# GpSimd makes the operands of the first merged projection alone: hi, lo and sums for 16 units beside attention heads 4 to 7

## The chip, the core and the metric

One core of one Trainium2 chip runs the whole program. The metric is device time in microseconds (us), the median of three runs; the profile is one more execution of the same program. The engines are TensorE (PE; its weight loads are PEld), VectorE (DVE), ScalarE (ACT), GpSimd (POOL) and the queue engine SyncE (SP). Each runs its own list of instructions strictly in order and waits for the others by semaphores.

## The reference

One encoder layer is applied to two groups of 512 tokens (g = 0, 1) with shared weights, model width 1024, all in float32. Cut to the part around the change:

```
h   = rmsnorm(x, g_mix);  u = h @ w_in          # columns feed both branches and the gates
hm  = mlstm(...)                                # 4 heads, both directions
y_m = (sigmoid(o) * rmsnorm(hm)) @ w_mo         # "first merged projection"
y_a = softmax_attention(q, k, v) @ w_ao         # 8 heads, 128 + 64 wide scores
x   = x + (sigmoid(g_m) * y_m + sigmoid(g_a) * y_a) @ w_out
x   = x + (silu(h2 @ w_gate) * (h2 @ w_up)) @ w_down ;  x = x + sigmoid(x @ w_ple_gate) * (p @ w_ple)
```

## The kernel before, in words

Every large product is made of float32 parts: an operand is split into a rounded part `hi` (a cast, on ScalarE) and the rest `lo` (operand minus hi, on VectorE, helper `lo_of`, L152), and three matmuls hi·hi, hi·lo, lo·hi are added up. A tile is 128 partitions by 512 columns.

The stages in order are: the first projection with the mLSTM heads, the attention (8 heads; each head is done for g = 0 and then g = 1, called half-heads here), then a chain of merged projections (w_mo, then w_ao), w_out, the gated network and the end. In the attention a half-head has, for four blocks of 128 queries, scores (`sc`, L742 to L746), a row maximum on VectorE (L748), an exponential on ScalarE (L751), a scaling of `p` (L754 on ScalarE, L756 on VectorE for one block in four), transposes (`pt`, L759), the split of the transposed block (`aph` on ScalarE, L761; `apl` on VectorE), and then the product with v (`av`, L766 to L768). Beside it stands the preparation of the same half-head of the next head: projections (`pj`), the rotary part on VectorE for every second head (`rope`, L691 to L698, then L723 and L724), the splits of q, k (`qnl`, `knl`) and of v, whose lo part (`vnl`) runs on GpSimd.

A merged projection multiplies a 2 by 2 block matrix of weights with a 2 by 2 block matrix of operands (`a`, `b` for one half of the channels in the two groups, `c`, `d` for the other half) in seven products instead of eight. The class `Ops` makes the operands of the products P1 (a), P2 (c), P7 (b - d), P6 (b - d - a), P5, Q4 and P3, for k = 0 to 3 in each. One (product, k) is called a unit. `Ops.need` makes a unit: `part` gives the source (a load of `hzd`, for P7 and P6 with a subtraction, L805 and L808), then hi, then lo (L827 to L830). For the first merged projection the 16 units of P1, P2, P7, P6 are made inside the attention: `HOPS` says how many after each half-head (3 after each of heads 4 and 5, 2 after each of head 6), and the loop at L968 draws them from the list `units`. Their raw tiles go through four buffers (two of `H`, tag rs, and two of `EV`, tag bk). The other twelve units (P5, Q4, P3) come when the chain starts; their raw tiles (again 16 loads of `hzd`) go to the pool `X2`, which opens in head 7. `Seven` makes the weights of the seven products: it loads two weight blocks from ScalarE's queue (`wst`), makes sums on GpSimd (L869 to L879) and splits them (`wp`, L843 and L152). The function `chain` asks for weights and operands a few products ahead.

The order on each engine isn't the order of the code: outside of pinned stretches a scheduler sets it when the program is built, from the dependences and its own estimates, and the pools decide which buffer a load has to wait for.

Of the kernel before, what the change touches and what calls it, by code (L numbers as in the profile page):

```python
# [62 lines left out]
def encoder_kernel(ctx: ExitStack, tc: tile.TileContext, a):  # L63
# [3 lines left out]
    class Engine:  # L67


        def __init__(self, e):  # L70
            self.e = e
# [13 lines left out]
    V, S, E, GP = (Engine(e) for e in (nc.vector, nc.scalar, nc.tensor, nc.gpsimd))  # L85
# [65 lines left out]
    def lo_of(out, src, hi, e=V):  # L151
        e.tensor_tensor(out=out, in0=src, in1=hi.bitcast(F32), op=ALU.subtract)  # L152
# [183 lines left out]
    for g in range(G):  # L336
# [3 lines left out]
        for d in range(2):  # L340
            for i in range(2):
                lo = 64 + 32 * i + 4 * d
# [74 lines left out]
    for i in range(NB):  # L417
        c = slice(i * P, (i + 1) * P)
        V.tensor_tensor_scan(
            out=M[:, c], data0=A[0][:, c], data1=A[0][:, c], initial=mprev[:, i : i + 1], op0=ALU.max, op1=ALU.max  # L420
# [4 lines left out]
    for d in range(1, NB):  # L425
        GP.tensor_copy(out=A[d][:, (NB - d) * P : T], in_=A[0][:, (NB - d) * P : T])
        for j in range(NB - d):
            e = (j + d) * P - 1
            V.tensor_scalar(
                out=A[d][:, j * P : (j + 1) * P],  # L430
# [13 lines left out]
    for d in range(NB + 1):  # L444
        src = A[d] if d < NB else em
# [196 lines left out]
    def merge_gate(name, dst, c):  # L642
        w = w8(f"{name}{c}")
        for g in range(G):
            t = hproj(w, g, EV("bk", "tg"))
            S.activation(out=t, in_=t, func=AF.Tanh, scale=0.5)
            nc.sync.dma_start(dst[g][c], t)
# [20 lines left out]
    for half in range(2):  # L668
        whi, wlo = weight(a["wv"][half])
        for g in range(G):  # L670
            for i in range(NB):
                bk = bank()
                for k in range(2):
                    n = slice(T * k, T * k + T)
                    hi, lo = (x[:, i * P : (i + 1) * P] for x in lat["ckv"][g][k])
# [40 lines left out]
    def attn_proj(hd, g, wa):  # L716
        if hd % 2 == 0:
            r = rope(proj1(wa, lat["cq"][g], 2, 0, "pj"), 4)
            st0 = Q("qst", "qs0", F32R)
            st1 = Q("qst", "qs1", F32R)  # L720
            S.copy(st0[0:64], r[0:64])
            S.copy(st1[64:128], r[64:128])
            V.tensor_tensor(out=st0[64:128], in0=r[0:64], in1=st0[0:64].bitcast(F32), op=ALU.subtract)  # L723
            V.tensor_tensor(out=st1[0:64], in0=r[64:128], in1=st1[64:128].bitcast(F32), op=ALU.subtract)  # L724
            qst[g] = [st0, st1]
        qn = split(proj1(wa, lat["cq"][g], 2, 256, "pj"), Q, "qkv", "qn")
        kn = split(proj1(wa, lat["ckv"][g], 2, 512, "pj"), Q, "qkv", "kn")
        vt = Q("tr", "avt")
        c = hd % 4 * P
        nc.sync.dma_start(vt.rearrange("p (a b) -> p a b", a=NB), vd[g][hd // 4].rearrange("a p c -> p a c")[:, :, c : c + P])  # L730
        vn = split(vt, Q, "qkv", "vn", GP)
        return qn, kn, vn, qst[g][hd % 2]
# [50 lines left out]
    def op(name, n, dt):  # L783
        return (H if name in ("P1", "P2", "P7", "P6") else late["OP"])("h", n, dt)

    class Ops:
# [1 line left out]


        def __init__(self, raw, tmp, sums):  # L790
            self.raw, self.tmp, self.sums = raw, tmp, sums
            self.r, self.t, self.x = {}, {}, {}

        def get(self, n, k):
# [26 lines left out]
        def need(self, name, ks=range(4)):  # L821
            x = self.x.setdefault(name, [])
            for k in ks:
                if len(x) == k:
                    src = self.part(name, k)
                    hi = op(name, "xh", F32R)
                    S.copy(hi, src)  # L827
                    lo = op(name, "xl", F32R)
                    lo_of(lo, src, hi)
                    x.append((hi, lo))  # L830

    wpn, wsn = [0], [0]
# [124 lines left out]
        raws[0] += 1  # L957
        return load(hzd[g][k], *stage[raws[0] % 4])

    hops = Ops(hraw, None, lambda n: V if n == "P7" else GP)  # L960
    hops.tmp = lambda: None
    units = [(n, [k]) for k in range(4) for n in ("P1", "P2", "P7", "P6")]

# [4 lines left out]
    for hd in range(AH):  # L968
# [7 lines left out]
        for g in range(G):  # L976
            attn(hd, g, ops[g])
            if hd < AH - 1:
                ops[g] = attn_proj(hd + 1, g, wa)
            for _ in range(HOPS.get((hd, g), 0)):  # L980
                hops.need(*units.pop(0))
        for _ in range(BULK[2 + hd]):
            merge_gate(*bulk.pop(0))
    assert not bulk
    Q.close()
    late["OP"] = Slots("OP", h=24, sg=4, ev=8)

# [34 lines left out]
    for g in range(G):  # L1022
        for k in (0, 4, 1, 5, 2, 6, 3, 7):
            t = yr[g][k]
            hi = H("h", "yh", F32R)
            S.activation(out=hi, in_=t, func=AF.Copy, scale=0.5)
            lo = H("h", "yl", F32R)
# [304 lines left out]


LEAD = 2
HOPS = {(4, 0): 3, (4, 1): 3, (5, 0): 3, (5, 1): 3, (6, 0): 2, (6, 1): 2}
LATN = (3, 0)
BULK = [10, 2, 1, 1, 1, 1, 0, 0, 0, 0]

# [92 lines left out]
```

## Time and profile before

| | us |
|---|---|
| median of 3 runs (lowest, highest) | 1901.08 (1899.88, 1902.36) |
| the profiled execution's own time | 1901.91 |
| its span, first to last instruction | 1900.0 |
| PE busy | 1843.9 (97% of the span) |
| DVE busy | 1235.4 (65%) |
| ACT busy | 879.3 (46%) |
| POOL busy | 466.8 (25%) |
| mean granted TensorE clock | 0.993 |

Busy is the time in which an engine had an instruction running. PE is close to full over the whole span, so time can only be lost or won where it stands idle or where its clock is lowered; idle time of the other engines costs nothing by itself. The sixteen units lie between about 740 and 790 us of the span, the attention ends and the merged chain begins at about 868 us.

### The profile page before, as it was taken

What the parts mean: (1) busy time and instruction counts of PE and PEld (TensorE: products, weight loads), DVE (VectorE), ACT (ScalarE), POOL (GpSimd) and SP (SyncE); (2) the same over time, 40 slices, a digit from 0 to 9 for tenths busy, and PEclk for the clock granted to TensorE, in tenths of its full rate; (3) what the DMA queues carried; (4) which work ended last, traced back from release to release, by engine and by line L of the source; (5) the groups of instructions that cost most, each with busy time, mean ns of one, the idle gap of its engine ahead of it and who ended that gap; (6) DMA issues with size and microseconds to landing.
All of it is one profiled execution on the core that took longest, in us unless ns stands there. A gap on an engine that the chain in (4) does not pass through costs nothing.

```text
span 1900.0 us, 24519 instructions
## 1 busy us (share of the span) xinstructions
PE 1843.9 (97%) x8840; PEld 1534.3 (81%) x8840; DVE 1235.4 (65%) x2153; ACT 879.3 (46%) x1711; POOL 466.8 (25%) x334
## 2 busy tenths in 40 slices
PE   7999999999999998999999998999999999999997
PEld 6888998988888877777877887888888887887886
DVE  7656575836556567976897586444444558878757
ACT  5255554644444565775534355333333344434442
POOL 3000000100000000233350035666465652322100
PEclk9999999999999999999999999999999999999998
DMA  4111111112253113345555241232223346534232
GB/s 164 51 45 34 57 34 56 34 67 73 78 177 133 57 64 117 102 142 201 162 193 183 89 167 60 90 123 99 97 98 102 120 142 228 162 127 136 89 126 89
DMA packets 98169, 207.59 MB, mean 109 GB/s; under 512 B 10688, under 2 KB 21312, under 8 KB 98048
## 3 DMA queue, kind: packets, MB, share of 16 engines
q1 hardware_dynamic: 85952, 163.03, 25.5%
q10 hardware_dynamic: 12096, 43.00, 7.0%
q8 instruction: 69, 1.13, 0.2%
q14 instruction: 52, 0.43, 0.1%
HBM read 151.89 MB, written 54.10 MB: 108 GB/s over the span
## 4 chain that ended last, share of the span: by engine, by line
PE 84%; DVE 10%; ACT 3%; DMA 2%; issue 2%; SPq 0%; DVEq 0%; ACTq 0%
PE b L894 12%; PE b L896 12%; PE b L895 12%; PE mm L183 8%; PE mm L181 8%; PE mm L182 8%; PE nm L580 3%; PE mm L79 2%; DVE xl L152 2%; PE mm L495 2%; PE mm L497 2%; PE mm L496 2%; DVE wp L152 1%; PE mm L1241 1%; PE mm L1243 1%
## 5 line engine op out<-in xcount | busy, mean ns | idle before, releaser
L894 PE MATMUL b<-xh,wp 128*128 128x512 f32 x1148 | 443.1, 394 | 9.9 <-ACT wp L843 4.4
L896 PE MATMUL b<-xh,wp 128*128 128x512 f32 x1148 | 445.0, 392 | 7.6 <-DVE wp L152 7.6
L895 PE MATMUL b<-xl,wp 128*128 128x512 f32 x1148 | 448.9, 392 | 0.0
L843 ACT CAST wp<-wst 128x512 fp32r<-128x512 f32 (+1 forms) x270 | 164.1, 612 | 307.5 <-PE b L896 251.4
L152 DVE TENSOR_TENSOR wp<-wst,wp 128x512 fp32r<-128x512 f32 (+1 forms) x270 | 239.4, 888 | 76.2 <-ACT wp L843 75.9
L894 PEld LDWEIGHTS b<-xh,wp 128*128 128x128 f32 x1148 | 216.5, 189 | 63.1 <-ACT wp L843 9.0
L896 PEld LDWEIGHTS b<-xh,wp 128*128 128x128 f32 x1148 | 216.6, 189 | 56.1 <-DVE wp L152 8.9
L895 PEld LDWEIGHTS b<-xl,wp 128*128 128x128 f32 x1148 | 216.5, 189 | 46.3
L181 PE MATMUL mm<-hh,whi 128*128 128x512 f32 x592 | 233.1, 394 | 7.3 <-ACT whi L166 7.0
L183 PE MATMUL mm<-hh,wlo 128*128 128x512 f32 x592 | 232.7, 395 | 2.3 <-DVE wlo L152 2.2
L182 PE MATMUL mm<-hl,whi 128*128 128x512 f32 x592 | 233.1, 394 | 0.3 <-DVE hl L277 0.3
L869 POOL TENSOR_TENSOR s<-wst,wst 128x512 f32<-128x512 f32 (+1 forms) x42 | 64.8, 1543 | 426.1 <-DMA wst<-w 171.6
L934 DVE TENSOR_TENSOR u<-b,u 128x512 f32<-128x512 f32 x90 | 61.5, 688 | 144.4 <-PE b L896 88.1
L181 PEld LDWEIGHTS mm<-hh,whi 128*128 128x128 f32 x592 | 112.4, 190 | 31.0 <-ACT whi L166 7.0
L183 PEld LDWEIGHTS mm<-hh,wlo 128*128 128x128 f32 x592 | 112.2, 190 | 26.4 <-DVE wlo L152 3.4
L182 PEld LDWEIGHTS mm<-hl,whi 128*128 128x128 f32 x592 | 112.2, 189 | 24.0 <-DVE hl L277 0.9
L166 ACT CAST whi<-wst 128x1024 fp32r<-128x1024 f32 (+1 forms) x71 | 73.0, 1029 | 104.3 <-PE mm L182 68.9
L152 DVE TENSOR_TENSOR xl<-ld,xh 128x512 fp32r<-128x512 f32 x121 | 94.9, 813 | 11.7 <-ACT xh L1176 6.8
L152 DVE TENSOR_TENSOR wlo<-wst,whi 128x1024 fp32r<-128x1024 f32 (+1 forms) x71 | 87.0, 1226 | 23.4 <-ACT whi L166 23.1
L929 ACT COPY u<-b 128x512 f32<-128x512 f32 x90 | 50.8, 588 | 107.6 <-PE b L896 80.2
L152 POOL TENSOR_TENSOR vnl<-avt,vnh 128x512 fp32r<-128x512 f32 x16 | 21.4, 1335 | 306.5 <-ACT vnh L156 283.8
L872 POOL TENSOR_TENSOR wst<-wst,wst 128x512 f32<-128x512 f32 (+1 forms) x42 | 78.6, 1873 | 39.2 <-DVE wp L152 29.9
(338 smaller groups left out, 3567.1 us busy)
## 6 DMA issues: line engine op xcount, KB each, us to landing
wst<-w SPq DMA_DIRECT2D x75, 512.0 KB
wst<-w ACTq DMA_DIRECT2D x60, 512.0 KB
ld<-actd SPq DMA_DIRECT2D x77, 256.0 KB
actd<-t SPq DMA_DIRECT2D x44, 256.0 KB
actd<-sg SPq DMA_DIRECT2D x33, 256.0 KB
x<-x SPq DMA_DIRECT2D x32, 256.0 KB
ld<-hzd SPq DMA_DIRECT2D x32, 256.0 KB
wst<-wd ACTq DMA_DIRECT2D x16, 512.0 KB
```

What stands on the lines that cost most here:

```text
L152: e.tensor_tensor(out=out, in0=src, in1=hi.bitcast(F32), op=ALU.subtract)
L166: S.copy(hi[:, :n], st[:, :n])
L181: E.matmul(bk, whi[:, c], hi, start=k == 0, stop=False)
L182: E.matmul(bk, whi[:, c], lo, start=False, stop=False)
L183: last_mm[0] = E.matmul(bk, wlo[:, c], hi, start=False, stop=k == nk - 1)
L843: S.copy(hi, src)
L869: GP.tensor_tensor(out=src, in0=a11, in1=a21, op=ALU.add)
L872: GP.tensor_tensor(out=a11, in0=a11, in1=a21, op=ALU.add)
L894: E.matmul(bk, whi[:, c], hi, start=bool(first) and k == 0, stop=False, **sk)
L895: E.matmul(bk, whi[:, c], lo, start=False, stop=False, **sk)
L896: E.matmul(bk, wlo[:, c], hi, start=False, stop=k == self.kh - 1, **sk)
L934: V.tensor_tensor(out=t, in0=b, in1=t, op=ALU.add if name == "P2" else ALU.subtract)
```

## The change

`Ops` gets a field `parts`. Where it names an engine, that engine makes both hi (as a copy with a cast) and lo; for the first merged projection it is GpSimd, which also takes the subtraction of P7 that VectorE had. The sixteen units are spread as two per half-head over heads 4 to 7, eight times two. Before the chain starts the field is taken back and the raw tiles are forgotten, so P5, Q4 and P3 use ScalarE and VectorE as before. Since the loop switches the loads to `X2` in head 7, the four units of k = 3 now read from `X2` too.

```
         def __init__(self, raw, tmp, sums):
-            self.raw, self.tmp, self.sums = raw, tmp, sums
+            self.raw, self.tmp, self.sums, self.parts = raw, tmp, sums, None
...
                     hi = op(name, "xh", F32R)
-                    S.copy(hi, src)
+                    if self.parts:
+                        self.parts.tensor_copy(out=hi, in_=src)
+                    else:
+                        S.copy(hi, src)
                     lo = op(name, "xl", F32R)
-                    lo_of(lo, src, hi)
+                    lo_of(lo, src, hi, self.parts or V)
...
-    hops = Ops(hraw, None, lambda n: V if n == "P7" else GP)
+    hops = Ops(hraw, None, lambda n: GP)
+    hops.parts = GP
...
     assert not bulk
+    hops.parts, hops.r, hops.t = None, {}, {}
...
-HOPS = {(4, 0): 3, (4, 1): 3, (5, 0): 3, (5, 1): 3, (6, 0): 2, (6, 1): 2}
+HOPS = {(hd, g): 2 for hd in range(4, 8) for g in range(2)}
```

VectorE before, at the start of the units (`xl` is the lo part of a unit, `ld` its raw tile, `apl` and `mx` belong to the attention, `rp` and `rs` to rope):

```order
L152 TENSOR_TENSOR xl_7482<-ld_7478,xh_7480 128x512
L749 TENSOR_SCALAR mx_7197<-mx_7197 128x1
L752 RECIPROCAL mx_7177<-mx_7177 128x1
L152 TENSOR_TENSOR knl_7121<-pj_7112,knh_7119 128x512
L805 TENSOR_TENSOR ld_7484<-ld_7484,ld_7486 128x512
L152 TENSOR_TENSOR xl_7491<-ld_7484,xh_7489 128x512
L152 TENSOR_TENSOR apl_7130<-pt_7144,aph_7129 128x4x128
L752 RECIPROCAL mx_7197<-mx_7197 128x1
L691 TENSOR_TENSOR rp_7234<-pj_7227,cos 128x512
L695 TENSOR_TENSOR rs_7236<-pj_7227,sin 32x512 x4
L152 TENSOR_TENSOR apl_7130<-pt_7164,aph_7129 128x4x128
```

VectorE now, at the same place:

```order
L752 RECIPROCAL mx_7177<-mx_7177 128x1
L749 TENSOR_SCALAR mx_7197<-mx_7197 128x1
L152 TENSOR_TENSOR knl_7121<-pj_7112,knh_7119 128x512
L152 TENSOR_TENSOR apl_7130<-pt_7144,aph_7129 128x4x128
L752 RECIPROCAL mx_7197<-mx_7197 128x1
L152 TENSOR_TENSOR apl_7130<-pt_7164,aph_7129 128x4x128
L691 TENSOR_TENSOR rp_7234<-pj_7227,cos 128x512
L695 TENSOR_TENSOR rs_7236<-pj_7227,sin 32x512 x4
```

The subtraction L805 and the lo parts that stood ahead of the attention's `apl` and of rope are gone from VectorE's list.

GpSimd before, at the end of the attention (`vnl` of the last half-head, then sums for P5, L811, and Q4, L817 and L818):

```order
L152 TENSOR_TENSOR vnl_8244<-avt_8240,vnh_8242 128x512
L811 TENSOR_TENSOR ld_8533<-ld_8533,ld_8535 128x512
L817 TENSOR_TENSOR ld_8582<-ld_8582,ld_8506 128x512
L817 TENSOR_TENSOR ld_8592<-ld_8592,ld_8515 128x512
L817 TENSOR_TENSOR ld_8602<-ld_8602,ld_8524 128x512
L818 TENSOR_TENSOR ld_8582<-ld_8582,ld_8585 128x512
L817 TENSOR_TENSOR ld_8612<-ld_8612,ld_8533 128x512
L818 TENSOR_TENSOR ld_8592<-ld_8592,ld_8595 128x512
L818 TENSOR_TENSOR ld_8602<-ld_8602,ld_8605 128x512
L818 TENSOR_TENSOR ld_8612<-ld_8612,ld_8615 128x512
L879 TENSOR_TENSOR wst_8622<-wst_8622 128x512
```

GpSimd now, the last part of the same stretch (`xl_8453` is P7 for k = 3, `ld_8446` its raw tile, `xh_8456` and `xl_8458` are P6 for k = 3):

```order
L152 TENSOR_TENSOR xl_8453<-ld_8446,xh_8451 128x512
L817 TENSOR_TENSOR ld_8612<-ld_8612,ld_8533 128x512
L818 TENSOR_TENSOR ld_8582<-ld_8582,ld_8585 128x512
L818 TENSOR_TENSOR ld_8592<-ld_8592,ld_8595 128x512
L818 TENSOR_TENSOR ld_8602<-ld_8602,ld_8605 128x512
L808 TENSOR_TENSOR ld_8446<-ld_8446,ld_8336 128x512
L818 TENSOR_TENSOR ld_8612<-ld_8612,ld_8615 128x512
L828 CAST xh_8456<-ld_8446 128x512
L882 TENSOR_TENSOR wst_8622<-wst_8622 128x512
L152 TENSOR_TENSOR xl_8458<-ld_8446,xh_8456 128x512
```

Between the `vnl` of the last half-head and the last Q4 sum (`ld_8612` by L818) there were 8 instructions; now there are 19, seven of them for the k = 3 units.

ScalarE before, in the first products of the chain (`u` copies a bank out; `wp` is the hi part of a weight, `wp_8802` that of P1 in the third pair of blocks; `wst_8780` its weight load):

```order
L827 CAST xh_8674<-ld_8615 128x512
L929 COPY u_8642<-b_1493_8491 128x512
L843 CAST wp_8744<-s_1556_8741 128x512
L855 DMA wst_8780<-w 128x1024
L929 COPY u_8660<-b_1538_8647 128x512
L843 CAST wp_8761<-wst_8484 128x512
L855 DMA wst_8782<-w 128x1024
L929 COPY u_8693<-b_1493_8491 128x512
L843 CAST wp_8785<-wst_8622 128x512
L843 CAST wp_8802<-wst_8780 128x512
```

ScalarE now, at the same place (`xh_8618` is the hi part of Q4 for k = 3, made from `ld_8612`):

```order
L830 CAST xh_8618<-ld_8612 128x512
L830 CAST xh_8662<-ld_8585 128x512
L858 DMA wst_8780<-w 128x1024
L830 CAST xh_8666<-ld_8595 128x512
L830 CAST xh_8670<-ld_8605 128x512
L830 CAST xh_8674<-ld_8615 128x512
L846 CAST wp_8761<-wst_8484 128x512
L858 DMA wst_8782<-w 128x1024
L846 CAST wp_8802<-wst_8780 128x512
L932 COPY u_8642<-b_1493_8491 128x512
```

The cast `wp_8802`, which needs the load `wst_8780`, now stands ahead of three `u` copies that it followed before; on PE its first matmul is the 73rd of the chain instead of the 133rd.

## Rows read from the trace of the kernel before

**Rows 1.** Windows: start:end, length, busy of each engine (instructions), granted clock, DMA share, GB/s.

```profile
743.00:867.00 124.00, 109.02 (x521) 85.23 (x520) 98.91 (x205) 90.55 (x187) 40.65 (x31) 0.99 0.37 120
743.00:760.00 17.00, 10.83 (x52) 8.03 (x51) 12.62 (x23) 9.89 (x21) 2.55 (x2) 1.00 0.50 151
760.00:769.00 9.00, 9.00 (x38) 7.30 (x37) 8.74 (x17) 6.65 (x15) 1.40 (x1) 0.81 0.59 177
761.00:762.00 1.00, 1.00 (x4) 0.81 (x3) 0.94 (x4) 0.93 (x2) 0.00 (x0) 0.50 0.50 104
769.00:777.00 8.00, 4.71 (x24) 3.36 (x23) 6.80 (x13) 6.38 (x14) 5.50 (x4) 1.00 0.35 110
800.00:850.00 50.00, 47.32 (x230) 37.35 (x229) 39.74 (x88) 37.88 (x79) 11.75 (x9) 1.00 0.28 97
867.00:900.00 33.00, 33.00 (x146) 27.19 (x145) 24.81 (x32) 15.78 (x29) 7.63 (x5) 1.00 0.69 248
```

**Rows 2.** Timeline, PE: start, length, instruction, [idle before it, and who released it].

```profile
750.07 0.50 PE L742 MATMUL sc<-knh,qnh 128*128 128x512 f32 x1 [1.69 <-ACT p L751]
...
759.24 0.50 PE L181 MATMUL pj<-ckvh,whi 128*128 128x512 f32 x1 [2.02 <-DVE mx L749]
...
775.54 0.66 PE L759 MATMUL pt<-ident,p 128*128 128x128 f32 x4 [1.94 <-ACT p L754]
...
815.83 0.50 PE L181 MATMUL pj<-cqh,whi 128*128 128x512 f32 x1 [1.08 <-DVE rs L695]
```

**Rows 3.** Timeline, DVE and ACT, units that wait for their load.

```profile
747.02 0.69 DVE L805 TENSOR_TENSOR ld<-ld,ld 128x512 f32<-128x512 f32 x1 [3.00 <-DMA ld<-hzd]
...
770.32 0.81 DVE L805 TENSOR_TENSOR ld<-ld,ld 128x512 f32<-128x512 f32 x1 [1.20 <-DMA ld<-hzd]
...
747.75 0.62 ACT L827 CAST xh<-ld 128x512 fp32r<-128x512 f32 x1 [3.32 <-DVE ld L805]
```

**Rows 4.** Groups by line and form, 690 to 860 us: busy, mean ns, idle before.

```profile
L152 DVE TENSOR_TENSOR xl<-ld,xh 128x512 fp32r<-128x512 f32 x16 | 10.7, 680 | 0.9 <-ACT xh L827 0.9
L805 DVE TENSOR_TENSOR ld<-ld,ld 128x512 f32<-128x512 f32 x4 | 2.9, 718 | 4.2 <-DMA ld<-hzd 4.2
L827 ACT CAST xh<-ld 128x512 fp32r<-128x512 f32 x16 | 9.6, 623 | 6.0 <-DVE ld L805 3.3 <-DVE wlo L152 2.2 <-DMA ld<-hzd 0.5
```

**Rows 5.** Timeline, POOL and DVE at the same time, and alone.

```profile
762.85 1.40 POOL L808 TENSOR_TENSOR ld<-ld,ld 128x512 f32<-128x512 f32 x1 [12.41 <-DVE xl L152]
...
763.03 2.03 DVE L152 TENSOR_TENSOR wlo<-wst,whi 128x768 fp32r<-128x768 f32 x1
...
789.80 0.96 DVE L152 TENSOR_TENSOR wlo<-wst,whi 128x768 fp32r<-128x768 f32 x1 [0.56 <-ACT whi L166]
...
749.17 1.28 POOL L808 TENSOR_TENSOR ld<-ld,ld 128x512 f32<-128x512 f32 x1 [3.39 <-DVE xl L152]
...
750.13 0.67 DVE L691 TENSOR_TENSOR rp<-pj,cos 128x512 f32<-128x512 f32 x1
```

**Rows 6.** Groups by line and form, POOL, whole span.

```profile
L808 POOL TENSOR_TENSOR ld<-ld,ld 128x512 f32<-128x512 f32 x4 | 5.2, 1310 | 19.3 <-DVE xl L152 15.8 <-DVE mx L749 1.9 <-issue 1.6
...
L426 POOL COPY A<-A 64x384 f32<-64x384 f32 x1 | 0.5, 498 | 0.0
```

**Rows 7.** Timeline of ACT, POOL, PE where the attention ends.

```profile
848.02 0.61 ACT L156 CAST vnh<-avt 128x512 fp32r<-128x512 f32 x1
...
852.53 3.78 POOL L817 TENSOR_TENSOR ld<-ld,ld 128x512 f32<-128x512 f32 x3
...
867.68 0.39 PE L894 MATMUL b<-xh,wp 128*128 128x512 f32 x1
...
879.93 0.34 ACTq L855 DMA_DIRECT2D wst<-w  x1
...
883.45 0.33 ACTq L855 DMA_DIRECT2D wst<-w  x1
...
888.62 1.44 POOL L869 TENSOR_TENSOR s<-wst,wst 128x512 f32<-128x512 f32 x1 [11.07 <-DMA wst<-w]
```

## The prediction

> **What bounds the kernel now.** I read the busy shares first: PE is busy 97% of the span, so the change can only act where PE is idle or slowed. I then cut the attention's second half into windows. From 743 to 867 us PE is busy 109.02 of 124.00, so 15.0 us are idle there, and in the chain behind it, 867 to 900, none of 33.00 [rows 1]. The idle time is not even. 743 to 760 loses 17.00 - 10.83 = 6.2 us and 769 to 777 loses 8.00 - 4.71 = 3.3 us: 9.5 us of the 15.0 lie in the 34 us where the units are made. 800 to 850 has the same attention work without units and loses 50.00 - 47.32 = 2.7 us [rows 1]. Between the two bad windows, 760 to 769, PE is never idle and yet does little: the granted clock is 0.81 on average and 0.50 at 761, the lower of its two levels (1.2 of 2.4 GHz), right after the idle spell [rows 1].
>
> The PE timeline then says who ended the waits: ScalarE's exponential (1.69 us at 750), VectorE's small steps (2.02 us at 759), ScalarE's scaling of p (1.94 us at 775) [rows 2]. Both engines had been held up by units. At 744 VectorE stood 3.00 us at the subtraction L805 because its load had not landed; ScalarE stood 3.32 us at the cast of the same unit, with the attention's next exponential behind it; at 769 the same happens for 1.20 us [rows 3]. What was queued behind then ran late, together with rope and further lo parts. So what bounds this stretch is VectorE and ScalarE working in order through instructions that are not urgent.
>
> **The change, part by part.** Taken off VectorE: 16 lo parts, 10.7 us, and 4 subtractions, 2.9 us, with 4.2 us of standing for loads. Taken off ScalarE: 16 casts, 9.6 us, with 6.0 us of standing [rows 4]. The number of `hzd` loads stays. For PE the gain is read from the two windows: 9.5 us idle, less what is idle without units. The hop-free rate is 2.7 us in 50, for 34 us 1.8 us; it fits the single wait for rope that is left in that window, 1.08 us at 815 [rows 1, 2], and rope stays. That gives 7.7 us. With the idle spell the low clock goes as well: 9.00 us at 0.81 is 1.7 us of work not done [rows 1]. Term A: -7.7 - 1.7 = -9.4 us. Its ends: -11.2 if nothing is left, -4.2 if only the standing for loads goes and VectorE's queue is as late as before.
>
> Added on GpSimd: 16 casts and 20 two-input instructions (16 lo parts, 4 subtractions; the 4 of P6 were there). A two-input one takes 1.31 us. The trace has no one-input cast of this shape; the nearest row, a copy of 384 columns in 498 ns, scaled to 512 columns gives 0.66 us, with ends 0.50 us (that row as it is) and 1.31 us (as two inputs) [rows 6]. The sum is 16 x 0.66 + 20 x 1.31 = 36.8 us (34 to 47) on an engine that is busy 40.65 of the 124 us [rows 1]. It fits: with some 115 us left to the stretch GpSimd goes from a third to two thirds busy. What waits behind a unit on GpSimd is the lo part of v, which the attention uses a half-head or more later, so a few us late costs nothing there. The loads' wait moves from VectorE to GpSimd and hides in its free third.
>
> The price is that the two engines are not independent. VectorE's `wlo` of 768 columns takes 0.96 us alone, and 2.03 us when it meets a GpSimd subtraction that began 0.18 us earlier: it starts when GpSimd is done. A VectorE instruction that reads PSUM, L691, ran in its 0.67 us beside another such subtraction [rows 5]. So only instructions of VectorE with all operands in SBUF pay: per half-head the scaling of p, and for some the weight's lo part and three of rope; with the weights of the first products, about 25 by the code. GpSimd's share rises by 36.8 / 115 = 0.32, and the mean wait is half of 1.31 us: 25 x 0.32 x 0.65 = 5.2 us on VectorE. Not all of it is PE's: VectorE is busy only 39.74 of 50 us without units, and the 2.03 us one was followed by a window in which PE had no idle [rows 1, 5]. Ends 0 and +5.2; I take +1.5, near the row that cost nothing. Term B: +1.5 us.
>
> The Trainium skill, page "SBUF — State Buffer", section "Who interferes with whom", says this as a rule: GpSimd shares a port pair with VectorE, and a VectorE instruction with two SBUF inputs, or in a two-port mode, and a GpSimd instruction that reads SBUF block each other wholly, whichever begins first, while one with at most one SBUF input goes on. This case's trace agrees, 2.03 against 0.96 us and 0.67 us undisturbed.
>
> Third, the entrance of the chain. GpSimd's list there is longer: after the last `vnl`, which can't start before ScalarE's cast ends at 848.6, 19 instructions stand ahead of the last Q4 sum instead of 8. With `vnl` and the sum itself these are 19 two-input ones at the back-to-back rate of 3.78 / 3 = 1.26 us and two casts at 0.66, 25.3 us in all: 873.9, or 6.2 us after the chain's first matmul at 867.68 [rows 7]. VectorE's run of lo parts for P5 at that time holds GpSimd up by some 2 us more, so about +8 us. ScalarE waits for that sum, and behind it stands the load of the third pair's weights: it is issued at about +10 us, where it was at 879.93, +12.2 us. It takes at least as long as the second one, 888.62 - 883.45 = 5.2 us, and at most 888.62 - 879.93 = 8.7 us [rows 7]; with the cast the weight is there at +16 to +19.5 us. PE is at its first matmul after 72 others, at 33.00 / 146 = 0.226 us each [rows 1]: +16.3 us. Before, it came after 132, at +29.8 us, with much room. So PE waits 0 to 3 us there, and ScalarE's `u` copy that frees the bank of P5 stands behind the same cast. Term C: +2.5 us; ends 0 (load on time) and +6 (sum 3 us later still). The k = 3 units themselves are in time: P7's lo part is done six instructions before the last Q4 sum, at about +0 us, and is wanted after 34 matmuls, +7.7 us; P6's is done 3.3 us after that sum, at about +11 us, and is wanted at +16 us.
>
> The chain behind is set by PE (33.00 of 33.00 busy) and its loads are issued by its own progress, so what is won before should arrive at the end. Sum: -9.4 + 1.5 + 2.5 = -5.4 us on the profiled execution's 1901.91 (span 1900.0), that is 1896.5 by its own time; it stood 0.8 us above the median, and from the median 1901.08 the sum is 1895.7 us.
>
> **The rivals.** First, the entrance eats the gain: the last Q4 sum is not +8 but +13 us late, because GpSimd gets in only between VectorE's instructions; the load goes out at +15, PE stands about 7 us at the 73rd matmul, and a low clock follows such an idle spell as it does at 761 [rows 1]: another 1.6 us. -9.4 + 1.5 + 8.6 = +0.7 us, 1901.8. For it: ScalarE's order, in which one late sum holds all. Against it: VectorE itself needs the Q4 sums and so leaves room.
>
> Second, the units were not the cause: the waits at 750 to 776 belong to rope and the latency of the softmax, and only the standing for loads goes: -4.2 + 1.5 + 1 = -1.7 us, 1899.4. For it: rope's instructions lie in the same 743 to 760 window. Against it: 800 to 850 has rope too and loses 2.7 us.
>
> Third, slower: the lock decides. GpSimd works in long back-to-back rows, so an instruction of VectorE that meets one waits almost a whole 1.31 us, and the 25 meet one in most cases, since GpSimd is two thirds busy: 25 x 0.66 x 1.31 = 21.6 us on VectorE. Without units VectorE has 50 - 39.74 = 10.3 us in 50, 24 us in 115, to spare [rows 1]; since it is the chain maximum, exponential, scale, split that PE waits for, about two thirds of the waits would reach it: 14 us against 9.4, with the entrance's 2.5 about +7 us, 1908. It decides from about 10 us of such waits on PE's path. For it: 2.03 us for 0.96 [rows 5]. Against it: the row with the full wait cost PE nothing. The Trainium skill, page "Perfetto Trace Analysis", section "Optimizing Scalar/DVE Operations", warns in this sense that moving operations between these two engines might not help; the trace bears out the wait and not, so far, its effect on PE.
>
> **How the numbers follow.** Forecast 0.54 (-5.4 us, between -11.2 + 0 and -4 us, 1890 to 1897); entrance 0.17; not the cause 0.14; lock 0.15. A measurement of this kernel tells about 0.2%, 3.8 us. The forecast case is faster by that bound nearly always (0.52) and the entrance case sometimes (0.03); no change: the rest of the forecast, most of the entrance and all of the second rival, 0.29; slower: the lock and the worst of the entrance, 0.16. The range takes in term A's full end with B and C at little (1889.5) and leaves out the lock's worse half: up to 1905. The likeliest case alone is 1890 to 1897.
>
> **What would show it.** Right: PE idle between 743 and 777 falls from 9.5 us to about 2, the clock is 1.00 throughout, VectorE and ScalarE wait for no `hzd` load; GpSimd is about two thirds busy up to the chain; `wlo`, the scaling of p and L698 show lengths of 1.3 to 2 us more often; a wait of PE of 0 to 3 us 16 us into the chain, ended by ScalarE's cast of a weight. Wrong: idle PE in heads 4 to 7 still near 15 us with waits ended by VectorE instructions that were held by GpSimd; a wait of 5 us or more at the 73rd matmul; or the gain visible at 868 and gone at 1000, where it would have met a limit that I do not see.

## The result, and the profile after

The changed kernel takes 1908.66 us (median of 9 runs, 1903.53 to 1910.71) against 1902.36 us of the kernel before on the same chip: a ratio of 1.0026, interval 1.0018 to 1.0034 (the two medians alone give 1.0033). It is slower by about 0.3%, where 1895.7 us was forecast. The profiled execution is the slowest of the nine, 1910.71 us, its span 1908.9 us.

The windows of the changed kernel come first, with the columns of [rows 1] (length, PE, PEld, VectorE, ScalarE, GpSimd, granted clock, DMA share, GB/s):

```profile
743.00:760.00 17.00, 15.36 (x75) 12.23 (x74) 13.22 (x25) 10.30 (x21) 10.90 (x10) 1.00 0.60 175
760.00:769.00 9.00, 7.88 (x39) 6.03 (x38) 7.22 (x17) 6.91 (x15) 7.70 (x7) 1.00 0.55 175
769.00:777.00 8.00, 8.00 (x46) 6.71 (x44) 5.25 (x13) 7.16 (x16) 6.56 (x7) 1.00 0.14 33
777.00:800.00 23.00, 20.28 (x92) 16.09 (x90) 19.43 (x38) 15.63 (x32) 14.55 (x13) 0.90 0.29 92
867.00:900.00 33.00, 28.85 (x120) 23.11 (x119) 25.39 (x30) 11.15 (x20) 12.92 (x9) 0.95 0.64 217
950.00:1000.00 50.00, 44.58 (x179) 35.14 (x178) 47.79 (x66) 21.43 (x38) 17.14 (x11) 0.93 0.58 190
```

For two of these windows, the same stretch in the kernel before:

```profile
777.00:800.00 23.00, 22.75 (x112) 18.34 (x112) 21.36 (x47) 18.23 (x39) 6.76 (x5) 1.00 0.33 104
950.00:1000.00 50.00, 47.64 (x207) 38.30 (x206) 48.77 (x64) 20.39 (x37) 26.80 (x11) 1.00 0.56 184
```

From 743 to 777 us the idle time of PE fell from 9.5 to 2.8 us (34.00 less 15.36, 7.88 and 8.00), and the stretch at the low clock is gone from there [rows 1], though 777 to 800 now has 0.90 where it had 1.00. So the attention did get faster. But PE, busy 33.00 of 33.00 us at the entrance of the chain before, now loses 4.2 us there and clock as well, and it loses 3 us and clock again after 950. The PE timeline of the changed kernel names the waits (start, length, instruction, [idle before, releaser]):

```profile
793.99 0.50 PE L742 MATMUL sc<-knh,qnh 128*128 128x512 f32 x1 [1.80 <-ACT p L751]
...
883.12 0.50 PE L897 MATMUL b<-xh,wp 128*128 128x512 f32 x1 [4.15 <-ACT wp L846]
...
962.46 0.62 PE L898 MATMUL b<-xl,wp 128*128 128x512 f32 x1 [2.64 <-DVE xl L152]
...
972.77 0.67 PE L897 MATMUL b<-xh,wp 128*128 128x512 f32 x1 [2.54 <-ACT wp L846]
```

The one at 883.12 is the 73rd matmul of the chain: the first of the third pair's P1, waiting for ScalarE's cast of its weight. The kernel before also waits twice where the projection's operands change, but shorter:

```profile
962.30 0.50 PE L894 MATMUL b<-xh,wp 128*128 128x512 f32 x1 [1.17 <-DVE xl L152]
...
966.99 0.50 PE L894 MATMUL b<-xh,wp 128*128 128x512 f32 x1 [1.19 <-ACT wp L843]
```

A count along the timeline shows how much is won and lost where. I take the time of the chain's 1st, 133rd and 601st matmul in both executions, and, because executions differ by up to 2 us before the units begin, subtract the offset at 641 us (1.05 us for the changed kernel) from the first of these columns. All 672 matmuls of the chain are recorded in each of these traces. The same count is given for every run below; minus is time won against the kernel before:

| kernel | median us | ratio, interval | attention | entrance, 1st to 133rd | 133rd to 601st |
|---|---|---|---|---|---|
| changed kernel | 1908.66 | 1.0026 (1.0018 to 1.0034) | -6.4 | +6.1 | +6.5 |
| e1 early | 1898.53 | 0.9975 (0.9966 to 0.9983) | -3.3 | 0.0 | +0.9 |
| e2 one in last head | 1897.34 | 0.9968 (0.9956 to 0.9980) | -5.8 | 0.0 | 0.0 |
| e3 old order of products | 1905.51 | 1.0012 (1.0000 to 1.0023) | -5.4 | +6.0 | +2.2 |
| e4 before, new order | 1916.82 | 1.0074 (1.0062 to 1.0086) | +0.1 | +3.7 | +9.3 |
| e5 Q4 sums on VectorE | 1904.47 | 1.0011 (1.0002 to 1.0019) | +0.4 | 0.0 | 0.0 |
| e6 casts only | 1902.87 | 0.9999 (0.9988 to 1.0010) | -0.9 | 0.0 | +1.0 |
| e7 lo parts only | 1896.28 | 0.9964 (0.9952 to 0.9977) | -6.9 | 0.0 | 0.0 |
| e8 last row on ScalarE, VectorE | 1898.16 | 0.9978 (0.9967 to 0.9990) | -6.4 | 0.0 | +0.7 |
| e9 spread alone, tiles kept | 1909.10 | 1.0028 (1.0017 to 1.0038) | +6.4 | 0.0 | 0.0 |
| e10 lo only, early | 1898.30 | 0.9975 (0.9966 to 0.9983) | -6.8 | 0.0 | +0.7 |
| e11 lo only, one in last head | 1895.84 | 0.9958 (0.9946 to 0.9971) | -9.3 | 0.0 | +0.8 |
| e12 old order, units and all sums held | 1913.20 | 1.0050 (1.0036 to 1.0064) | -9.7 | +17.6 | +0.6 |
| e13 units first | 1895.29 | 0.9960 (0.9948 to 0.9972) | -6.3 | 0.0 | 0.0 |
| e14 spread alone | 1910.74 | 1.0035 (1.0023 to 1.0047) | +6.3 | 0.0 | +0.1 |

The changed kernel wins 6.4 us in the attention and loses 12.6 us in two places behind it: 6.2 us in all, beside 6.3 us between the medians.

### The profile page after: what moved, and what is told of

Its sections match the earlier page's. It is cut to its first block, busy times and chain, and to the rows that moved or that the text cites. A ratio compares the mean times of both kernels' runs of the same rounds, so it can differ in the third digit from the quotient of the medians.

```text
span 1908.9 us, 24522 instructions
## 1 busy us (share of the span) xinstructions
PE 1849.1 (97%) x8840; PEld 1538.6 (81%) x8840; DVE 1236.9 (65%) x2133; ACT 872.7 (46%) x1695; POOL 497.4 (26%) x370
## 4 chain that ended last, share of the span: by engine, by line
PE 83%; DVE 10%; DMA 3%; ACT 2%; issue 2%; SPq 0%; ACTq 0%; DVEq 0%
PE b L897 12%; PE b L899 12%; PE b L898 12%; PE mm L183 8%; PE mm L181 8%; PE mm L182 7%; PE nm L580 3%; PE mm L79 2%; DVE xl L152 2%; PE mm L495 2%; PE mm L497 2%; PE mm L496 2%; DVE wp L152 1%; PE pt L759 1%; PE mm L1246 1%
## 5 line engine op out<-in xcount | busy, mean ns | idle before, releaser
L152 DVE TENSOR_TENSOR xl<-ld,xh 128x512 fp32r<-128x512 f32 x105 | 90.2, 892 | 10.7 <-ACT xh L1181 6.7
```

## The experiments

**e1 and e2: the same GpSimd work, ended sooner.** The edits are one line each; with both, the scheduler gives PE the order of products of the kernel before.

```
-HOPS = {(hd, g): 2 for hd in range(4, 8) for g in range(2)}
+HOPS = {(4, 0): 3, (4, 1): 3, (5, 0): 3, (5, 1): 3, (6, 0): 2, (6, 1): 2}                        # e1
+HOPS = {(4, 0): 3, (4, 1): 3, (5, 0): 2, (5, 1): 2, (6, 0): 2, (6, 1): 2, (7, 0): 1, (7, 1): 1}  # e2
```

> All sixteen units on GpSimd as in the changed kernel, but spread 3, 3, 3, 3, 2, 2 over the half-heads 4 to 6 as before, so that the last unit is done a head before the chain; the scheduler then gives PE the same order of the chain's products as in the kernel before. Theory O (the order: the changed kernel wins 6 us in the attention and loses 12.6 us behind it because its chain's products come in another order, the third pair's weights wanted at the 73rd matmul instead of the 133rd): the gain of the attention arrives at the end, 1894 to 1898 us, no wait of PE of over 1.5 us in the chain's first 20 us, waits at 955 to 975 as in the kernel before (about 2.4 us in all). Rival L (the lock between VectorE and GpSimd, and GpSimd's work as such): no gain, 1902 us or more, since the same 37 us of GpSimd work stand in fewer half-heads.

> As the changed kernel, all units on GpSimd, but 3, 3, 2, 2, 2, 2, 1, 1 over the eight half-heads: the last head still makes the last two units (P7 and P6 of the fourth row), only two earlier ones are no longer behind them. The scheduler gives the order of products of the kernel before. Theory O: 1895 to 1900 us, the third pair's weights wanted at the 133rd matmul, no wait there; a wait of 0 to 2 us for the last lo part of P6 at most. Rival L (lock and late GpSimd work): 1905 to 1909 us, as the changed kernel.

Both are faster than both kernels, by 0.25% and 0.32%. In e2 PE is ahead of the kernel before by 4.32 us by the traces' own times (5.8 with the offset) at every matmul from the 1st of the chain to the 385th: what reaches the chain does pass through it. e2 came in as theory O has it, and e1 0.5 us above its range. That GpSimd's work costs as such (rival L) does not hold, though e1 keeps only half of the gain of the attention. These two don't part the order from the late pieces, since both are gone in them; e3 and e4 do.

**e3 and e4: the order of the products alone.** The 56 products of the chain are written out in a fixed order and PE is held to it: the changed kernel in the old order (e3), the kernel before in the new one (e4). The loop that emits them becomes

```
-for at, (q, n) in enumerate(order):
-    ...
-    made[q].product(n)
+for at, n in SEGS:            # (product, matmuls), e.g. (6, 10), (5, 12), (6, 2)
+    ...
+    for _ in range(n):
+        next(run[at], None)   # product() yields after each matmul; PE is kept in program order
```

> The changed kernel with all its units where they are, but PE's matmuls of the chain written out in the order of the kernel before and held in it. Theory O: the attention's gain of 6 us stays; no wait for the third pair's weights; PE waits 2 to 4 us in the chain's first 15 us for the last lo part of P6, which GpSimd makes late (47th matmul); nothing is lost at 955 to 975 beyond the kernel before: 1897 to 1901 us. Rival R (the late operands: the order only follows them, and whatever the order, their lateness costs the same): 1906 to 1910 us.

> The kernel before with its engines and units, but PE's matmuls of the chain written out in the order of the changed kernel and held in it. Theory O: the order alone costs: a wait of 1 to 5 us at the 73rd matmul for the third pair's weights and 4 to 7 us more than before at 955 to 975: 1907 to 1914 us. Rival R (late operands): no operand is late here, so the order costs nothing: 1901 to 1903 us.

e4 is slower by 14 us, more than theory O had, with the units made as in the kernel before: the new order costs by itself, 3.7 us at the entrance, at the 73rd matmul, and 9.3 us behind it. These are its waits there:

```profile
953.77 0.79 PE L80 MATMUL b<-xh,wp 128*128 128x512 f32 x1 [3.82 <-ACT wp L844]
957.99 1.22 PE L80 MATMUL b<-xh,wp 128*128 128x512 f32 x2 [1.72 <-DVE wp L153]
```

They stand at the 338th and 343rd matmul, where the changed kernel loses nothing; its own loss lies between the 385th and the 441st. So e4 shows that the order can cost, not that it costs the changed kernel the same waits. In e3 the loss behind the 133rd matmul falls from 6.5 to 2.2 us, so most of that part of the changed kernel's loss goes with the order. Holding PE to an order was not tried by itself, but from the 61st to the 421st matmul e3 keeps step with the kernel before. At the entrance e3 still loses 6.0 us, at another matmul. This is PE in e3, and GpSimd's instruction that it waits for:

```profile
878.99 0.78 PE L80 MATMUL b<-xl,wp 128*128 128x512 f32 x1 [4.07 <-POOL xl L153]
```

```profile
875.63 1.64 POOL L883 TENSOR_TENSOR wst<-wst 128x512 f32<-128x512 f32 x1 [3.03 <-DVE wp L153]
877.23 1.71 POOL L153 TENSOR_TENSOR xl<-ld,xh 128x512 fp32r<-128x512 f32 x1
```

The last lo part of P6 (k = 3, the fourth row) is late in GpSimd's list, behind all sums of P5 and Q4, and behind a weight's sum that itself stood 3.03 us for VectorE. So the old order waits for the operand and the new one for the weight. Neither theory had it whole: O was right for most of the loss behind 950, rival R at the entrance.

**e5: a shorter list by moving the sums.** `hops = Ops(hraw, None, lambda n: V if n == "Q4" else GP)` instead of `GP` for all.

> The changed kernel, all units on GpSimd two per half-head to the end, with one line more: the eight two-input sums of Q4's operands go to VectorE instead of GpSimd. GpSimd's list at the entrance is eight instructions (about 10 us) shorter ahead of the last lo part of P6, and the scheduler gives PE the order of products of the kernel before. Theory Q (the lateness at the entrance is the length of GpSimd's list there: units and Q4 sums together, and the other order follows from it): no wait of PE of over 1 us in the first 30 us of the chain, the attention's gain of about 6 us stays, 955 to 975 as in the kernel before: 1895 to 1899 us. Rival L (the lock: GpSimd's units hold VectorE up, which now has 5 us more to do): waits ended by VectorE's lo parts of 2 to 5 us at the entrance, 1900 to 1905 us.

The entrance is clean and the scheduler comes back to the old order, as theory Q has it. The whole gain of the attention is lost, though, and not where rival L put it: ahead of the chain, where the sums now stand among the attention's last steps. PE in e5, then VectorE and GpSimd in the same time:

```profile
861.30 1.09 PE L759 MATMUL pt<-ident,p 128*128 128x128 f32 x4 [6.36 <-DVE apl L152]
```

```profile
854.47 1.73 DVE L818 TENSOR_TENSOR ld<-ld,ld 128x512 f32<-128x512 f32 x1
856.12 1.75 DVE L817 TENSOR_TENSOR ld<-ld,ld 128x512 f32<-128x512 f32 x1
...
863.65 0.68 DVE L817 TENSOR_TENSOR ld<-ld,ld 128x512 f32<-128x512 f32 x1
```

```profile
855.61 1.71 POOL L152 TENSOR_TENSOR xl<-ld,xh 128x512 fp32r<-128x512 f32 x1
857.40 1.60 POOL L808 TENSOR_TENSOR ld<-ld,ld 128x512 f32<-128x512 f32 x1
```

A sum on VectorE takes 0.68 us alone and 1.7 us while GpSimd is at its units; four of them, 854.47 to 860.5, stand ahead of the split that PE waits for. They take 6.2 us where 4 x 0.68 would be 2.7, so by this estimate about half of the 6.36 us is the lock, and the lock is on the path here; the rest is the sums themselves.

**e6 and e7: the two halves of the change.** e6 leaves the lo parts on VectorE, e7 the casts on ScalarE:

```
-lo_of(lo, src, hi, self.parts or V)      +lo_of(lo, src, hi)       # e6
-self.parts.tensor_copy(out=hi, in_=src)  +S.copy(hi, src)          # e7
```

> Half of the change: GpSimd makes the sixteen casts (and the subtractions), VectorE keeps the sixteen lo parts. Spread 2 per half-head as in the changed kernel; order of products in the chain as in the kernel before. VectorE then stands behind a cast that itself waits for its load. Theory A (the attention lost its time because ScalarE and VectorE both worked in order through units that waited for loads): part of the gain, 743 to 777 us idle between 4 and 8 us, 1897 to 1901 us. Rival S (ScalarE's casts alone were the cause): the whole gain, idle 3.5 us as in the changed kernel, 1895 to 1897 us. Rival V (VectorE's lo parts alone): no gain, 1901 us or more.

> The other half of the change: GpSimd makes the sixteen lo parts (and the subtractions), ScalarE keeps the sixteen casts, which stand for the loads ahead of the attention's exponentials. Spread 2 per half-head as in the changed kernel; order of products in the chain as in the kernel before. Theory A (both engines): part of the gain, 743 to 777 us idle between 4 and 8 us, 1897 to 1901 us. Rival S (ScalarE's casts alone): no gain, 1901 us or more. Rival V (VectorE's lo parts alone): the whole gain, 1895 to 1897 us.

e7 has the whole gain (-6.9 us) and a clean entrance, as rival V has it. e6 reaches the chain with next to none, but it doesn't lack the gain where the forecast put it. These are 743 to 777 us in the kernel before, e6, e7 and e14 (the new spread alone, below):

```profile
743.00:777.00 34.00, 24.55 (x111) 18.69 (x110) 28.15 (x50) 22.92 (x47) 9.46 (x7) 0.95 0.49 148
743.00:777.00 34.00, 29.84 (x141) 24.05 (x140) 29.07 (x57) 21.70 (x46) 17.10 (x17) 0.95 0.45 144
743.00:777.00 34.00, 29.73 (x140) 22.68 (x140) 27.44 (x51) 25.15 (x52) 23.04 (x18) 1.00 0.49 146
743.00:777.00 34.00, 25.00 (x112) 18.87 (x110) 28.36 (x53) 22.62 (x46) 8.25 (x7) 0.95 0.50 155
```

PE's idle time there falls from 9.5 to 4.2 us in e6 and to 4.3 in e7. Counted at the attention's products with v, e6 is 4.7 us ahead at 850 us and loses 3.9 of it up to the chain, where VectorE has the last head's lo parts to make; e14, with the same spread, loses 9.9 us there. Against e14 the casts and subtractions win 7.2 us before the chain, the lo parts and subtractions 13.2, and all three 12.7. The subtractions of P7 moved in both halves, and no run moves them alone.

This is the group of VectorE's lo parts in e6, 740 to 860 us (busy, mean ns):

```profile
L152 DVE TENSOR_TENSOR xl<-ld,xh 128x512 fp32r<-128x512 f32 x14 | 14.8, 1060 | 0.1
```

They were 680 ns in the kernel before [rows 4]. In e6, where GpSimd makes the casts and subtractions in between, they take 0.38 us longer each, 5.3 us for 14. So e6 doesn't show that the casts were harmless on ScalarE. e7 shows it for the case in which VectorE's lo parts are gone: there ScalarE has all sixteen casts and the attention's gain is complete.

**e8: only the fourth row taken back.** `hops.parts = None` from the last head on.

> The changed kernel, but the four units of the fourth row (the last head's) have their casts on ScalarE and lo parts on VectorE as before; the other twelve stay on GpSimd. GpSimd's list ahead of the chain is eight instructions shorter, the order of products is that of the kernel before. Theory Q (length of GpSimd's list at the entrance): entrance without a wait of over 1 us, attention's gain mostly kept (the last head's units stand on ScalarE and VectorE, up to 2 us lost there): 1896 to 1900 us. Rival L (GpSimd's work in the attention costs as such): 1902 us or more.

As expected by Q: entrance clean, gain kept. Eight instructions fewer on GpSimd at that place are enough.

**e9 and e14: the spread alone.** The kernel before with two units per half-head over the last four heads. e9 kept the fourth row's tiles, so that its P5 and Q4 are made from other values of that row; e14 loads them again.

> The kernel before with its engines (casts on ScalarE, lo parts on VectorE, subtractions of P7 on VectorE) and only the new spread, two units per half-head over the last four heads. Theory V (the cause in the attention is the lo parts on VectorE, wherever they stand): no gain, 1900 to 1905 us, the idle time of 743 to 777 us partly moved to 777 to 867. Rival P (the spread, two instead of three per half-head, is what helps): 1896 to 1899 us.

> The kernel before with its engines and only the new spread, two units per half-head over the last four heads, and the fourth row's tiles loaded again for P5 and Q4 behind the attention as in the kernel before (the earlier run of the spread alone kept the tiles, so that its P5 and Q4 were made from other values of that row). Theory V (lo parts on VectorE are the cause, wherever they stand): no gain or a loss, 1901 to 1910 us. Rival P (the spread helps): 1896 to 1899 us.

On ScalarE and VectorE the new spread costs 6.3 us before the chain begins, more than theory V had for e9 (4 us above its range). It is 3.6 us ahead at 850 us and loses 9.9 us from there on. This is the end of the attention in e14:

```profile
850.00:867.00 17.00, 13.23 (x53) 9.76 (x52) 13.70 (x25) 10.05 (x22) 16.37 (x13) 0.80 0.71 234
```

Rival P is out: what the spread earns by itself up to 850 us it more than loses in the last head. With the lo parts on GpSimd it costs nothing that shows (-6.9 in e7, -6.8 with the old spread in e10).

**e10 and e11: lo parts on GpSimd with other spreads** (e7 with the two lines of e1 and e2).

> Only the lo parts and subtractions on GpSimd, casts on ScalarE, and the spread of the kernel before (3, 3, 3, 3, 2, 2, done a head before the chain). Theory V (lo parts on VectorE): gain as with the lo parts alone at two per half-head, 1894 to 1898 us, entrance without a wait. Rival P (the spread): three per half-head crowd the attention and ScalarE stands for their loads as in the kernel before: 1899 to 1902 us.

> Only the lo parts and subtractions on GpSimd, casts on ScalarE, spread 3, 3, 2, 2, 2, 2, 1, 1. The candidate for the fastest: theory V and Q both expect 1894 to 1897 us, attention's gain of 6 to 7 us kept through the chain. Rival P: 1898 us or more, because of the three per half-head.

e10 has the attention's gain and came in 0.3 us above theory V's range. e11 is faster than both kernels, 0.42% under the kernel before, and not to be told from e7 and e13 by these runs.

**e12 and e13: the place in GpSimd's list.** e12 holds PE to the old order and all of GpSimd's instructions of the last head and the entrance to program order, the weights' sums too; e13 holds only the operands' part and leaves PE to the scheduler. The core of e13:

```
+GP.p = hd == AH - 1          # GP.p: what GpSimd is given now is kept in program order
 hops.need(*units.pop(0))
+GP.p = False
...
+GP.p = not head and at < 5   # first five products of the chain
 quads[i][0].need(m)
+GP.p = False
```

> The changed kernel with PE's products held in the order of the kernel before, and in the last head GpSimd's instructions held in the order in which the program has them: the units of the fourth row first, the sums for P5 and Q4 behind them. Theory Q (P6's last lo part is late because the sums stand ahead of it in GpSimd's list): the wait of 4.1 us at the 47th matmul is gone (less than 1 us), the sums are about 8 us later but wanted only at the 133rd matmul: 1898 to 1901 us. Rival L (the lock between VectorE and GpSimd at the entrance, whatever the order): 2 to 4 us of waits remain at the entrance, 1903 to 1907 us.

> The changed kernel, whole, and only GpSimd's operand work at the entrance held in program order: the units of the fourth row first, the sums for P5 and Q4 behind them; the sums for weights stay free (in the run before, these were held too and the one for P6 came last). PE's order is the scheduler's own, and comes out as in the kernel before. Theory Q (P6's last lo part is late because sums stand ahead of it in GpSimd's list, and the other order of products follows from that): no wait of over 1 us in the chain's first 30 us, nothing lost at 955 to 975, 1895 to 1900 us. Rival L (the lock at the entrance, whatever the order): 2 to 5 us of waits remain there, 1901 to 1907 us.

e12 missed its range by 12 us and tells of another list error: with the weights' sums behind the operands' sums, the sum for P6's weight ran at 877.77 us, and PE waited 7.46 us for it. It settles nothing about P6's operand. e13 does. GpSimd in e13 (held instructions are recorded under the helper's line L80), and its windows:

```profile
849.27 0.61 POOL L80 CAST xh<-ld 128x512 fp32r<-128x512 f32 x1
...
853.46 1.28 POOL L80 TENSOR_TENSOR xl<-ld,xh 128x512 fp32r<-128x512 f32 x1
854.70 12.24 POOL L80 TENSOR_TENSOR ld<-ld,ld 128x512 f32<-128x512 f32 x9
870.58 1.67 POOL L883 TENSOR_TENSOR wst<-wst 128x512 f32<-128x512 f32 x1 [3.63 <-DVE wp L153]
872.21 4.82 POOL L80 TENSOR_TENSOR ld<-ld,ld 128x512 f32<-128x512 f32 x3
```

```profile
867.00:900.00 33.00, 33.00 (x146) 27.11 (x145) 23.33 (x31) 13.12 (x24) 14.29 (x8) 1.00 0.78 274
950.00:1000.00 50.00, 47.65 (x207) 38.25 (x206) 47.69 (x63) 20.89 (x38) 19.68 (x11) 1.00 0.59 194
```

The last lo part of P6 is done at 854.7 us instead of 877.1, the last sum of Q4 at 877.0 instead of 869.7, 15.6 us into the chain, and nobody waits. GpSimd's work is the same as in the changed kernel; its order, and the order of products that the scheduler then chooses, make 13.4 us (1908.66 less 1895.29, each beside a before of 1902.4 to 1902.6).

## Why the prediction was wrong

**Term A, -9.4 us.** Right in place, too large by 3 us. The 9.5 idle us of 743 to 777 became 2.8 and the low clock went, 8.4 us in all, as the words on what would show it said. But the forecast took the rate of the stretch without units for what is late next. What came next were waits at 792 to 796 for ScalarE's exponential and a lo part of q, with the clock at 0.90: PE does 20.28 of 23.00 us there instead of 22.75. Measured over the attention: -6.4. The attribution to both engines holds only in part. With VectorE's lo parts gone, ScalarE's casts and their standing [rows 3, 4] cost PE nothing that shows (-6.9 in e7, -6.4 with the casts moved too). With the lo parts left on VectorE, casts and subtractions still won 7.2 us against the same spread (e6, e14). The two don't add up, and which of them made the exponential late at 750 us was not separated.

**Term B, +1.5 us.** VectorE did get longer where both operands are in SBUF: in the changed kernel's groups of 690 to 862 us L724 takes 1082 ns (687 before), L723 752 (684) and L698 842 (682), four of each, 2.5 us together; `wlo` got shorter, 1120 for 1228 ns. It is part of the -6.4; how much of it PE felt was not measured, and the lo parts alone, with the same kind of lock, won 6.9. The Trainium skill's rule on the shared port (page "SBUF — State Buffer", section "Who interferes with whom"), that a VectorE instruction with two SBUF inputs and a GpSimd instruction that reads SBUF block each other, held again: 1060 for 680 ns in e6, 1.7 for 0.68 us in e5. The rival of the lock was wrong for this change in the attention, and right in e5, where the sums stood in the path.

**Term C, +2.5 us.** The place was right, the 73rd matmul, and the size was at its far end: 4.15 us of waiting and 1.7 us of low clock (the 12 matmuls after it took 4.43 instead of 2.72 us), 5.9 us of the 6.1 counted. The step that failed is the one that priced the third pair's load. It was put at +10 us, behind the last Q4 sum. That sum was even a little early, +7.3 us for +8; the load went out at +15.3. These are VectorE, ScalarE and GpSimd of the changed kernel there:

```profile
863.72 6.52 DVE L152 TENSOR_TENSOR xl<-ld,xh 128x512 fp32r<-128x512 f32 x4 [3.83 <-ACT xh L830]
...
875.88 1.78 DVE L152 TENSOR_TENSOR wp<-wst,wp 128x512 fp32r<-128x512 f32 x1
```

```profile
877.69 0.33 ACTq L858 DMA_DIRECT2D wst<-w  x1
878.07 1.66 ACT L830 CAST xh<-ld 128x512 fp32r<-128x512 f32 x3 [5.56 <-DVE wp L152]
...
882.45 0.62 ACT L846 CAST wp<-wst 128x512 fp32r<-128x512 f32 x1 [2.21 <-DMA wst<-w]
```

```profile
862.02 4.26 POOL L818 TENSOR_TENSOR ld<-ld,ld 128x512 f32<-128x512 f32 x3
...
869.63 1.07 POOL L828 CAST xh<-ld 128x512 fp32r<-128x512 f32 x1
873.74 1.67 POOL L882 TENSOR_TENSOR wst<-wst 128x512 f32<-128x512 f32 x1 [3.03 <-DVE wp L152]
875.37 1.74 POOL L152 TENSOR_TENSOR xl<-ld,xh 128x512 fp32r<-128x512 f32 x1
```

ScalarE stood 5.56 us, until VectorE had made the lo part of a weight at 877.66, and only then issued the load. VectorE, never idle from 863.72 on, was late most of all because its four lo parts of operands, met by GpSimd's sums, took 6.52 us. In the kernel before, where GpSimd stood still at that time, five took 3.10:

```profile
869.02 3.10 DVE L152 TENSOR_TENSOR xl<-ld,xh 128x512 fp32r<-128x512 f32 x5 [3.83 <-ACT xh L827]
```

I had counted the lock there on GpSimd's side only (2 us) and not on VectorE's. The rival "the entrance eats the gain" came within 3 us of this wait with the wrong instruction as its cause. P6's last lo part was mis-sized too: done at +14.7 us, not +11. The new order wants it late enough; the old one, in e3, waits for it.

**"What is won before should arrive at the end."** This step failed outright, and it is the largest part: +6.5 us between the 133rd and the 601st matmul, for which the sum had no term. It rested on a chain set by PE in the kernel before; but the change had also given PE another order of products. I had read that order only where its first consequence stood, the 73rd matmul, and not followed it to where the projection's operands change, 955 to 975. With the old order the step holds (e2, e13: constant through the chain); with the new one it fails even with all units on ScalarE and VectorE (e4), though at other matmuls. Why the new order costs there was not tried and stays open: VectorE is busy 47.79 of 50 us in the changed kernel and 48.77 before, so it has little room in either.

**The cause behind C and this step** is one: the fourth row's units stand behind the sums of P5 and Q4 in GpSimd's list (e13), and with them in that place the scheduler puts P6 off and pulls the third pair forward, and either order waits. That it is the place and not the amount of work is shown by e13; that fewer instructions there help as well, by e2, e7 and e8. With the list in order the time was 1895.29 us: the attention's 6.3 us arrive at the end and nothing is lost on the way. That this lies near the 1895.7 us forecast for the changed kernel is chance: the terms behind that sum are not the ones measured.

## What to carry to other kernels

Where a change moves work to an engine whose last pieces are wanted by the next stage, read that engine's whole list at the handover: what stands ahead of the last piece, and what each of those waits for. If the order of another engine changes with it, follow that order through every later stage in which an engine is full; a window without idle time in the old order says nothing about the new one. And price a move in halves: here the lo parts alone had all of the gain, and the casts, added to them, only lengthened the list.

## What the runs showed of the hardware

GpSimd's cast of a 128x512 tile took 0.61 us beside VectorE instructions that read PSUM (849.27 in e13) and 1.07 us at the entrance of the changed kernel (row at 869.63); the estimate had been 0.66. Where VectorE and GpSimd both work through rows of two-input instructions in SBUF, it is not only GpSimd that slows down: four lo parts of VectorE took 6.52 us, 1.63 each, where 0.68 is their time alone.
